# A macaron block on one core: the second FFN's down product partly by seven block products, and the gates' sigmoids moved to the reading back

## The chip, the cores and the metric

The kernel runs on one core of a Trainium2 chip. The core has a matrix engine (TensorE, PE in the profile, with its weight loads as PEld), VectorE (DVE), ScalarE (ACT), GpSimd (POOL) and SyncE (SP, which here only issues DMAs). Each engine works through its own list of instructions in order; semaphores between the lists make one wait for another. The metric is the time of one execution on the device in microseconds (us). Three runs of the kernel before gave 1213.32, 1214.26 and 1214.87 us; the median is 1214.26.

## The reference

One block for x of 512 tokens by 1024 channels, all in float32:

```python
x = x + 0.5 * swiglu(rmsnorm(x, norm_ffn1_g), ffn1_w_gu, ffn1_w_down)
x = x + hybrid_mixer(rmsnorm(x, norm_mix_g), w_in, conv_w, ...)
x = x + 0.5 * swiglu(rmsnorm(x, norm_ffn2_g), ffn2_w_gu, ffn2_w_down)
return rmsnorm(x, final_norm_g)

def swiglu(x, w_gu, w_down):
    g, u = jnp.split(x @ w_gu, 2, axis=-1)
    return (jax.nn.silu(g) * u) @ w_down        # 1024 -> 2 x 2816 -> 1024
```

The mixer projects x by w_in into the parts of a short convolution (cb, cc, cu), of a gated linear attention (q, k, v, a low-rank gate, r) and into two gates ga and gb. It ends with

```python
merged = jax.nn.sigmoid(ga) * y_conv + jax.nn.sigmoid(gb) * y_gla
return merged @ w_o
```

## The kernel before

**Precision.** Every float32 product is made of three products in the type fp32r: a value is split into a high part (a cast on ScalarE) and a low part (value minus high part, a subtraction on VectorE), and high·high, high·low and low·high are summed. So every tile of weights costs a cast (L292) and a subtraction (L293), 128x1024 each, before TensorE can use it, and activations are split in the same way.

**Weights.** The class `Weights` (L226) streams all weights in the order of two tables: PLAN lists units (blocks of a matrix, at most 128x1024 in one tile), STEPS says which unit is used when. A unit is loaded into a pool `f` of 10 buffers by a DMA on SP's queue (L266); it is cast and subtracted into the pools `wh` and `wl` (3 buffers each) two steps before its use. The last four units (TAIL) go into buffers of the pool `op` instead, which has 14.

**Sets.** A large product is done in sets: a 2x2 block product by seven block products instead of eight (a Strassen-Winograd form). Their names, in the order in which a set takes them, are m1, p2, q6, p5, q7, p4, p3; where sets follow one another, the next set's first products are put between the last ones of this set (`order`, L80). Each set's weights are four loaded units a11, a12, a21, a22 and a fifth buffer s3. Sums of them are made in place: s3 = a11 + a21 on VectorE (L279), and a21 += a22, a11 += a21, a12 += a11 by accumulating DMAs that GpSimd issues (L270), the first three steps ahead of m1, the others right behind the casts for m1 and p2. Set loads are issued six steps ahead. The activations' side (class `Operands`, L493) has seven operands of 128x1024: four of them sums made in place on VectorE (L512 to L519), each cast (L532) and subtracted (L533) into two `op` buffers. `Set.run` (L470) makes one product: 24 matmuls 128x256 (L484) into one of three banks. The products m1, q6, q7 and p4 accumulate in the same bank b, p2 in a, p5 and p3 in c; after m1, q6 and q7 ScalarE copies bank b out (L489).

**FFN2.** The up product is units of its own for the first pairs, then nine sets. After sets 0 to 7 TensorE transposes x back to tokens-by-channels (`natural`, L678). Then `last_down` (L686): for each of 22 k tiles (128 rows of the down matrix, one unit of 128x1024) 4 token blocks by 2 column halves by 3 products, 528 matmuls 128x512 in all (L699 to L701), which accumulate in 8 banks over all k. The hidden activations are split two k tiles at a time (`split_hid`, L644: cast L648, subtraction L649). The last four k tiles go block by block, with the residual, the final norm and the store after each (`part`, `store`).

**Mixer gates.** ga and gb are made by four sets among the twelve sets of w_in (MSETS, L122). When a quarter of one is done it is put together from banks and copies (`quarter`, L1139; for p4 straight from the bank), a sigmoid is taken on ScalarE (L1163; for p4 L1158), and it is stored to DRAM by a DMA that ScalarE issues (L1170). Later `gate` (L1210) reads it back by a DMA on SP's queue: ga for the eight outputs of w_out_conv (`for d in range(KD)`, L1230), gb for the two sets of w_out_gla. The attention's gate and the set of r need other functions on ScalarE (L908 to L929; Silu for r), and a change of function can need a load of a table (ACT_TABLE_LOAD).

A scheduler sets each engine's order from the program's order and estimated times, except in the last token blocks, where the order is written by hand (L756).

Of the kernel before, what the change touches and what calls it, by code (L numbers as in the profile page):

```python
# [15 lines left out]
P = 128  # L16
S = 512
# [45 lines left out]
def full(mat, kt):  # L63
    return [(mat, k, 1, (0,), 1024) for k in range(kt)]
# [58 lines left out]
         ("conv", 3), ("cb", 0), ("cb", 1), ("r", 0), ("r", 1)]  # L123


def ffn_plan(up, down, plain, slow):

    units(group(up, KD, (0, DFF, P, DFF + P), slow))
    for f in range(2, plain):
        units(single(up, KD, f * P))  # L130
        units(single(up, KD, DFF + f * P))
    sets(up, [(s * HW, DFF + s * HW) for s in range(plain // 2, KF // 2)])
    units(full(down, KF))
    ENDS.append(len(STEPS))


# [30 lines left out]
def block_kernel(ctx: ExitStack, tc: tile.TileContext, xT, vecs, gf, gup, wgl, wts, out):  # L167
# [371 lines left out]
    def run_sets(make, ahead=2, hooks={}):  # L539


        at = W.taken
        seq = []
        while STEPS[at + len(seq)][1] is not None:
# [12 lines left out]

    def ffn(up, down, norm, nxt, plain, at):
# [6 lines left out]

        o = mm_group(up, KD, (0, DFF, P, DFF + P), xh, xl, extra=finish, slow=nxt is not None)
        row = rows[0]
        xn = {}

        def normed(j, l):  # L570

            if (j, l) not in xn:
                t = slice(l * HW, (l + 1) * HW)
                v = tile_of("hid", [P, 1024]).rearrange("p (k t) -> p k t", t=HW)
# [10 lines left out]
        hid = []  # L585

        def plain_pair(f, g, u):
            if f % 2 == 0:
                hid.append(tile_of("hid", [P, 2, S]))
# [17 lines left out]
            plain_pair(f, g, u)  # L607

        def up_set(i):
            h = tile_of("hid", [P, 2, S])  # L610
            hid.append(h)

            def done(s, p):
                bank, v = s.bank, s.v
# [36 lines left out]

        us = full(down, KF)
        if nxt is None:
            return last_down(us, split_hid)
        o = [AUX(), AUX()] + [MM() for _ in range(KD - 2)]

        def mm(d, k, w, hl):
# [28 lines left out]
    def last_down(us, split_hid):  # L686
        X = XS[-1]
        gr = []
        for e in range(2):
            g = acc_row.tile([P, S], F32, tag=("acc", "row")[e], name=f"gr{e}")  # L690
# [5 lines left out]
        def mm(t, e, k, w, hl):  # L696
            wh, wl = (a[:, 512 * e : 512 * (e + 1)] for a in w)
            a, b = (v[:, k % 2, t * P : (t + 1) * P] for v in hl)
            nc.tensor.matmul(o[t][e], a, wh, start=k == 0, stop=False)  # L699
# [75 lines left out]
    def mixer(norm, nxt):  # L775
# [377 lines left out]
        def act_done(func, use):  # L1153

            def done(s, p):
                if p == "p4":
                    t = T()
                    nc.scalar.activation(t, s.bank["b"], func, scale=-1.0)  # L1158
                else:
                    t = quarter(s, p)  # L1160
                    if t is None:
                        return
                    nc.scalar.activation(t, t, func)  # L1163
                use(int(p in ("p4", "q7")), int(p in ("q7", "p3")), t)
            return done

        def gate_done(name, i):
            def use(a, l, t):
                d = 4 * i + 2 * a
                nc.scalar.dma_start(  # L1170
                    gates_d[name][d : d + 2, :, half(l)].rearrange("e p t -> p e t"), pair(t))
            return act_done(AF.Sigmoid, use)

        def r_done(i):
            def use(a, l, t):
# [34 lines left out]
        def gate(name, d, l=None, t=None):  # L1210

            t = T() if t is None else t
            if l is None:
                nc.sync.dma_start(t, gates_d[name][d])
            else:
                nc.sync.dma_start(pair(t), gates_d[name][d : d + 2, :, half(l)].rearrange(
                    "e p t -> p e t"))
            return t

        c_h, c_l = parts([Y[i][:, :, 2:] for i in range(4)])  # L1220
# [141 lines left out]
```

## Time and profile before

| | |
|---|---|
| time, median of three runs | 1214.26 us |
| span of the profiled execution | 1213.3 us |
| PE busy | 1198.3 us (99% of the span) |
| DVE busy | 788.4 us (65%) |
| ACT busy | 591.4 us (49%) |
| POOL busy | 94.9 us (8%) |
| DMA, read and written | 124.55 MB and 8.39 MB, 110 GB/s over the span |
| ScalarE's table loads | 1.28 us each |

The trace has the times of one execution; that span is 1213.3 us, and the median of the runs, which also takes in what lies around a span, is 1.0 us more. Matmuls overlap, so the duration of one (0.39 us for 128x512) is not what it costs; its cost is the distance from one start to the next. Instructions on DVE and ACT overlap by some 0.09 us in the same way.

### The profile page before, as it was taken

The page shows a single profiled execution, that of the slowest core. Times are in us where ns is not written, and L with a number is a line of the kernel's source. Part 1 is how long each engine was busy: PE and PEld are TensorE (multiplying, and loading weights), DVE is VectorE, ACT ScalarE, POOL GpSimd, SP SyncE. Part 2 cuts the span into 40 slices and gives each one's busy share as a digit, 9 for nine tenths or more (in the row PEclk, how much of TensorE's full clock was granted, in tenths as well). Part 3 has the DMA queues.
Part 4 walks back from the last instruction along what each step waited for, and adds up shares of the span by engine and source line. Part 5 has one row for each costly group of instructions (what it writes and reads, how often), then busy time and mean ns, then how long its engine had stood idle before and what let it go on. Part 6 is the DMA issues. An engine that isn't in the chain of part 4 may idle for free.

```text
span 1213.3 us, 19084 instructions
## 1 busy us (share of the span) xinstructions
PE 1198.3 (99%) x7882; PEld 1103.2 (91%) x7882; DVE 788.4 (65%) x944; ACT 591.4 (49%) x733; POOL 94.9 (8%) x131
## 2 busy tenths in 40 slices
PE   9999999999999999999999999999999999999997
PEld 7899999988888889998999998988889999998886
DVE  7976666732277765666778778676597656583325
ACT  6555455532154465857555463444356545562323
POOL 0011111000010000010101100200001111100000
PEclk9999999999999999998999999999999999999999
DMA  9477776521162326765777756751537777752201
GB/s 343 98 198 189 178 192 177 174 88 61 52 243 86 95 64 165 205 159 144 199 191 178 191 168 208 202 163 67 184 89 199 181 184 170 184 186 88 70 1 70
DMA packets 57767, 184.51 MB, mean 152 GB/s; under 512 B 6384, under 2 KB 12656, under 8 KB 57680
## 3 DMA queue, kind: packets, MB, share of 16 engines
q1 hardware_dynamic: 37936, 124.27, 29.0%
q0 software_dynamic: 15104, 54.53, 24.3%
q10 hardware_dynamic: 4640, 4.49, 1.1%
q8 instruction: 61, 1.00, 0.3%
q14 instruction: 26, 0.21, 0.1%
HBM read 124.55 MB, written 8.39 MB: 110 GB/s over the span
## 4 chain that ended last, share of the span: by engine, by line
PE 95%; DMA 2%; DVE 1%; ACT 1%; issue 1%; SPq 0%; POOL 0%; ACTq 0%; DVEq 0%; POOLq 0%
PE mm L484 50%; PE mm L344 7%; PE mm L322 6%; PE mm L320 6%; PE mm L321 6%; PE mm L701 2%; PE mm L699 2%; PE mm L700 2%; PE mm L362 1%; PE mm L363 1%; PE mm L361 1%; DMA f<-f 1%; PE aux L701 1%; PE aux L322 1%; PE aux L320 1%; PE aux L699 1%
## 5 line engine op out<-in xcount | busy, mean ns | idle before, releaser
L484 PE MATMUL mm<-op,wh 128*128 128x256 f32 x3584 | 652.1, 285 | 3.0 <-ACT tp L489 2.5
L292 ACT CAST wh<-f 128x1024 fp32r<-128x1024 f32 (+1 forms) x313 | 326.9, 1046 | 502.4 <-PE mm L484 218.8
L484 PEld LDWEIGHTS mm<-op,wh 128*128 128x128 f32 x3584 | 562.6, 193 | 4.3 <-ACT tp L489 2.7
L293 DVE TENSOR_TENSOR wl<-f,wh 128x1024 fp32r<-128x1024 f32 (+1 forms) x313 | 380.6, 1218 | 284.8 <-ACT wh L292 274.0
L484 PE MATMUL mm<-op,wl 128*128 128x256 f32 x1792 | 509.6, 285 | 2.6 <-DVE wl L293 2.5
L484 PEld LDWEIGHTS mm<-op,wl 128*128 128x128 f32 x1792 | 345.4, 193 | 3.0 <-DVE wl L293 3.0
L270 POOL DMA_DIRECT2D f<-f x96 | 82.9, 863 | 827.4 <-DVE wl L293 471.8
L320 PE MATMUL mm<-op,wh 128*128 128x512 f32 x324 | 126.5, 390 | 0.0
L322 PE MATMUL mm<-op,wl 128*128 128x512 f32 x324 | 126.3, 390 | 0.0
L321 PE MATMUL mm<-op,wh 128*128 128x512 f32 x324 | 126.1, 389 | 0.0
L322 PEld LDWEIGHTS mm<-op,wl 128*128 128x128 f32 x324 | 60.8, 188 | 12.7
L321 PEld LDWEIGHTS mm<-op,wh 128*128 128x128 f32 x324 | 60.9, 188 | 12.6
L320 PEld LDWEIGHTS mm<-op,wh 128*128 128x128 f32 x324 | 60.8, 188 | 12.4
L344 PE MATMUL mm<-op,wh 128*128 128x512 f32 x256 | 63.7, 391 | 0.6 <-DVE op L395 0.3
L344 PEld LDWEIGHTS mm<-op,wh 128*128 128x128 f32 x256 | 47.7, 188 | 11.4 <-ACT wh L292 0.9
L489 ACT COPY tp<-mm 128x512 f32<-128x512 f32 x96 | 55.6, 580 | 4.6 <-PE mm L484 4.6
L699 PE MATMUL mm<-wh,op 128*128 128x512 f32 x108 | 42.0, 389 | 0.0
L700 PE MATMUL mm<-wl,op 128*128 128x512 f32 x108 | 42.0, 389 | 0.0
L701 PE MATMUL mm<-wh,op 128*128 128x512 f32 x108 | 42.0, 389 | 0.0
L279 DVE TENSOR_TENSOR f<-f,f 128x1024 f32<-128x1024 f32 x32 | 39.2, 1224 | 0.8
L649 DVE TENSOR_TENSOR op<-hid,op 128x1024 fp32r<-128x1024 f32 x22 | 26.9, 1222 | 17.7 <-ACT op L648 17.7
L344 PE MATMUL mm<-op,wl 128*128 128x512 f32 x128 | 34.4, 390 | 0.0
(252 smaller groups left out, 1129.0 us busy)
## 6 DMA issues: line engine op xcount, KB each, us to landing
f<-wts SPq DMA_DIRECT2D x219, 512.0 KB, 4.1
f<-f POOLq DMA_DIRECT2D x96, 512.0 KB, 4.9
X<-xT SPq DMA_DIRECT2D x8, 256.0 KB, 6.1
xs<-X POOLq DMA_DIRECT2D x8, 256.0 KB, 5.6
ga<-tp ACTq DMA_DIRECT2D x8, 256.0 KB, 2.7
gb<-tp ACTq DMA_DIRECT2D x8, 256.0 KB, 4.0
g<-gb SPq DMA_DIRECT2D x8, 256.0 KB, 5.0
tp<-ga SPq DMA_DIRECT2D x8, 256.0 KB, 5.9
```

The costliest lines, as they stand in the source:

```text
L270: nc.gpsimd.dma_start(out_, a, accum_op=ALU.add)
L292: nc.scalar.copy(h[:, :w], raw[:, :w])
L293: nc.vector.tensor_tensor(out=l[:, :w], in0=raw[:, :w], in1=h[:, :w].bitcast(F32), op=ALU.subtract)
L320: nc.tensor.matmul(o, wh, ah, start=first, stop=False)
L321: nc.tensor.matmul(o, wh, al, start=False, stop=False)
L322: nc.tensor.matmul(o, wl, ah, start=False, stop=last)
L344: nc.tensor.matmul(o[c], w[:, s : s + P], a[k], start=k == 0 and j == 0, stop=k == kt - 1 and j == 2)
L484: nc.tensor.matmul(to, ww[:, s], aa[:, t], start=fresh and k == 0 and e == 0 and j == 0, stop=k == 3 and j == 2, skip_group_check=True)
L489: nc.scalar.copy(v, o)
L699: nc.tensor.matmul(o[t][e], a, wh, start=k == 0, stop=False)
L700: nc.tensor.matmul(o[t][e], a, wl, start=False, stop=False)
L701: nc.tensor.matmul(o[t][e], b, wh, start=False, stop=k == KF - 1)
```

## The change

Two things. First, k tiles 0 to 15 of FFN2's down product are done by two sets (`wide_sets`), each over 8 k tiles, both column halves and all 512 tokens. A block is 4 k tiles by 512 columns by 256 tokens; as it has twice the size of a block in the other sets, each of the seven products takes two units of weights and 24 matmuls 128x512, and accumulates in two banks of 128 tokens each. 2 x 7 x 24 = 336 matmuls stand where 16 x 24 = 384 stood. The set's results are halved and summed straight into x: ScalarE copies bank b out with a factor of 0.5 after m1, q6 and q7 (L756 of the new kernel), VectorE adds the second bank (L759, L764, L773) or adds to x itself (L769), and GpSimd adds the sum into x (L761, L766, L775). k tiles 16 to 21 stay as they were. The products here come in the order of SEQ, without another set's products between. The pool of hidden activations is divided otherwise: two buffers of 16 KB a partition for the wide sets, three of 4 KB.

Second, the gates ga and gb are stored without their sigmoid (for p4 a Copy with scale -1 remains), and `gate` takes it after the reading back, in place.

```diff
+WIDE = 2
+SEQ = ("m1", "p2", "q6", "p5", "q7", "p4", "p3")
+def wide_sets(mat):
+    for w in range(WIDE):
+        subs = []
+        for u in range(2):
+            subs.append(len(PLAN))
+            PLAN.extend((mat, 8 * w + 4 * j + 2 * u, 2, (512 * c,), 512)
+                        for c in range(2) for j in range(2))
+        for p in SEQ:
+            STEPS.extend((n, p) for n in subs)
...
-    units(full(down, KF))
+    if not slow:
+        wide_sets(down)
+    units(full(down, KF)[0 if slow else 8 * WIDE :])
...
+        def run_wide(w):
+            ops = Operands(lambda j, l: wides[w][:, 4 * j : 4 * j + 4, l * HW : (l + 1) * HW])
+            bank, v = {}, {}
+            for at, p in enumerate(SEQ):
+                for q in SEQ[at : at + 2]:
+                    ops.make(q)
...
+                o = bank[b]
+                bh, bl = ops.get(p)
+                for u in range(2):
+                    h, l = W.take()
+                    for i in range(2):
+                        k = 2 * u + i
+                        wh, wl = (a[:, i * 512 : (i + 1) * 512] for a in (h, l))
+                        for t in range(2):
...
+                for t in range(2):
+                    if p in ("m1", "q6", "q7"):
+                        v.setdefault(p, []).append(T())
+                        nc.scalar.activation(v[p][t], o[t], AF.Copy, scale=0.5)
+                    if p == "p2":
+                        y, x_ = v["m1"][t], block(0, 0)[:, t]
+                        nc.vector.scalar_tensor_tensor(out=y, in0=o[t], scalar=0.5, in1=y,
+                                                       op0=ALU.mult, op1=ALU.add)
+                        nc.gpsimd.tensor_tensor(out=x_, in0=x_, in1=grid(y), op=ALU.add)
...
+                    if p == "p4":
+                        x_ = block(1, 0)[:, t]
+                        nc.vector.scalar_tensor_tensor(out=x_, in0=grid(o[t]), scalar=-0.5, in1=x_,
+                                                       op0=ALU.mult, op1=ALU.add)
...
-        for k in range(KF - TAIL):
+        K0 = 8 * WIDE
+        for k in range(K0, KF - TAIL):
...
-                    nc.scalar.activation(t, s.bank["b"], func, scale=-1.0)
+                    nc.scalar.activation(t, s.bank["b"], func or AF.Copy, scale=-1.0)
...
-                    nc.scalar.activation(t, t, func)
+                    if func is not None:
+                        nc.scalar.activation(t, t, func)
...
-            return act_done(AF.Sigmoid, use)
+            return act_done(None, use)
...
+            nc.scalar.activation(t, t, AF.Sigmoid)
             return t
...
-    FFN = dict(f=10, hid=11, tp=9)
+    FFN = dict(f=10, hidw=2, hid=3, tp=9)
```

Lines move: in the weights' class L292 and L293 become L310 and L311 and the GpSimd DMA L270 becomes L288; the operands' L532 and L533 become L550 and L551; the copy L489 becomes L507; in the mixer L1163, L1158 and L1170 become L1256, L1250 and L1263, and the new sigmoid is L1311.

The lists of instructions change in three places that the prediction speaks of. The first is ScalarE in the mixer's sets, where the second ga set is made beside the attention's gate. Before, from the copy of a bank on (`wh` are casts of weights, `tp` quarters of a gate, `g` and `sm` the attention's gate, `mm` and `aux` banks):

```order
L489 COPY tp_5217<-mm_5187 128x512
L292 CAST wh_5219<-f_4602 128x1024
L1158 ACT_TABLE_LOAD
L1158 ACTIVATE tp_5247<-mm_4911 128x512
L292 CAST wh_5253<-f_4862 128x1024
L1170 DMA ga<-tp_5247 128x2x256
L292 CAST wh_5283<-f_4866 128x1024
L925 ACT_TABLE_LOAD
L925 ACTIVATE sm<-g_506_3628 128x8
L1163 ACT_TABLE_LOAD
L1163 ACTIVATE tp_5311<-tp_5311 128x512
L926 ACT_TABLE_LOAD
```

The same place after the change:

```order
L507 COPY tp_5204<-mm_5174 128x512
L310 CAST wh_5206<-f_4593 128x1024
L1017 ACT_TABLE_LOAD
L1017 ACTIVATE sm<-g_497_3623 128x8
L1018 ACTIVATE sm<-g_497_3623 128x8
L1019 ACTIVATE g_500_3626<-g_498_3624 128x512
L1250 ACTIVATE tp_5234<-mm_4900 128x512
L310 CAST wh_5240<-f_4851 128x1024
L1263 DMA ga<-tp_5234 128x2x256
L1020 ACTIVATE g_498_3624<-g_498_3624 128x512
L310 CAST wh_5270<-f_4855 128x1024
```

Three table loads of this stretch are gone, and the sigmoid of a ga quarter with them; one table load stands between the first two casts of weights still, and the attention's gate has moved forward.

The second place is ScalarE from the end of the last r set to the first outputs of w_out_conv. Before (L1202 casts the convolution's result, L532 the attention's):

```order
L489 COPY tp_7053<-mm_6870 128x512
L292 CAST wh_7059<-f_6610 128x1024
L1202 CAST op_7177<-y_3402 128x1024
L1163 ACTIVATE tp_7055<-tp_7055 128x512
L292 CAST wh_7099<-f_7091 128x1024
L1163 ACTIVATE tp_7088<-tp_7088 128x512
L292 CAST wh_7132<-f_7093 128x1024
L1158 ACTIVATE tp_7128<-mm_6870 128x512
```

After, the first gb gate's sigmoid comes ahead of the copy, and again some rows on, ahead of the weights of the fourth output (the second fence):

```order
L1311 ACT_TABLE_LOAD
L1311 ACTIVATE g_497_3623<-g_497_3623 128x512
L507 COPY tp_7036<-mm_6853 128x512
L310 CAST wh_7042<-f_6593 128x1024
L1295 CAST op_7160<-y_3397 128x1024
L1256 ACT_TABLE_LOAD
L1256 ACTIVATE tp_7038<-tp_7038 128x512
L1256 ACTIVATE tp_7071<-tp_7071 128x512
L310 CAST wh_7082<-f_7074 128x1024
```

The rows that follow four rows later, still on ScalarE (two sigmoids of ga after one of gb and one Silu of r):

```order
L1311 ACT_TABLE_LOAD
L1311 ACTIVATE g_499_3625<-g_499_3625 128x512
L1256 ACT_TABLE_LOAD
L1256 ACTIVATE tp_7144<-tp_7144 128x512
L1311 ACT_TABLE_LOAD
L1311 ACTIVATE tp_7173<-tp_7173 128x512
L1311 ACTIVATE tp_7220<-tp_7220 128x512
L310 CAST wh_7226<-f_7080 128x1024
```

Sigmoids that wait for a reading back, and the changes of table between them and the Silu of r, now stand ahead of casts of weights; before the change there was no table load here.

The third place is ScalarE in the first wide set, around the evacuation of q7 (`hidw` is the set's block of hidden activations; L550 casts its operands):

```order
L310 CAST wh1502_10961<-f1434_10558 128x1024
L550 CAST op1534_11151<-hidw1186_8664 128x1024
L310 CAST wh1506_10982<-f1426_10518 128x1024
L310 CAST wh1508_11000<-f1433_10556 128x1024
L550 CAST op1536_11156<-hidw1186_8664 128x1024
L756 ACTIVATE tp1510_11016<-mm1462_10796 128x512
L756 ACTIVATE tp1511_11020<-mm1463_10797 128x512
L310 CAST wh1514_11030<-f1424_10514 128x1024
```

VectorE at that place:

```order
L311 TENSOR_TENSOR wl1507_10983<-f1426_10518,wh1506_10982 128x1024
L532 SCALAR_TENSOR_TENSOR hidw1186_8664<-hidw1186_8664 128x4x256
L311 TENSOR_TENSOR wl1509_11001<-f1433_10556,wh1508_11000 128x1024
L537 SCALAR_TENSOR_TENSOR hidw1186_8664<-hidw1186_8664 128x4x256
L764 SCALAR_TENSOR_TENSOR tp1510_11016<-mm1488_10925,tp1510_11016 128x512
L764 SCALAR_TENSOR_TENSOR tp1511_11020<-mm1489_10926,tp1511_11020 128x512
L311 TENSOR_TENSOR wl1515_11031<-f1424_10514,wh1514_11030 128x1024
```

Before, this stretch held a cast and a subtraction of one unit for each k tile and a `split_hid` for every two. Now the two copies of bank b (mm1462 and mm1463) stand on ScalarE behind the cast of an operand (op1536), whose input the sum L532 on VectorE makes; TensorE's product p4 writes the same two banks.

More of the change, by code (lines that the diff above doesn't have):

```diff
@@ L543, in run_sets @@
         seq = []
-        while STEPS[at + len(seq)][1] is not None:
+        while STEPS[at + len(seq)][1] is not None and PLAN[STEPS[at + len(seq)][0]][4] == HW:
             seq.append(STEPS[at + len(seq)])
@@ L567, in ffn @@
         row = rows[0]
-        xn = {}
+        xn, xn_tile = {}, []
         def normed(j, l):
@@ L573, in normed @@
                 t = slice(l * HW, (l + 1) * HW)
-                v = tile_of("hid", [P, 1024]).rearrange("p (k t) -> p k t", t=HW)
+                if not xn:
+                    xn_tile.append(tile_of("hidw", [P, 4, 4, HW]))
+                v = xn_tile[0][:, len(xn)]
                 for i in range(4):
@@ L585, in ffn, with new_hid @@
         hid = []
+        wides = []
+        def new_hid():
+            i = len(hid)
+            if i < 4 * WIDE:
+                if i % 4 == 0:
+                    wides.append(tile_of("hidw", [P, 8, S]))
+                hid.append(wides[-1][:, 2 * (i % 4) : 2 * (i % 4) + 2])
+            else:
+                hid.append(tile_of("hid", [P, 2, S]))
+            return hid[-1]
         def plain_pair(f, g, u):
             if f % 2 == 0:
-                hid.append(tile_of("hid", [P, 2, S]))
+                new_hid()
             s, t = T(), T()
@@ L609, in up_set @@
         def up_set(i):
-            h = tile_of("hid", [P, 2, S])
-            hid.append(h)
+            h = new_hid()
             def done(s, p):
@@ L653, in ffn @@
         if nxt is None:
-            return last_down(us, split_hid)
+            return last_down(us, split_hid, wides)
         o = [AUX(), AUX()] + [MM() for _ in range(KD - 2)]
@@ L684, in natural, with last_down, block, grid @@
         nc.scalar.copy(X[:, i], o)
-    def last_down(us, split_hid):
+    def last_down(us, split_hid, wides):
         X = XS[-1]
+        def block(c, l):
+            return X[:, 4 * c : 4 * c + 4, l * HW : (l + 1) * HW].rearrange(
+                "p d (t i) -> p t d i", i=P)
+        def grid(t):
+            return t.rearrange("p (d i) -> p d i", i=P)
+        def run_wide(w):
[4 more added lines that the diff above has]
+                    ops.make(q)
+                b = {"m1": "b", "p2": "a", "q6": "b", "p5": "c", "q7": "b", "p4": "b",
+                     "p3": "c"}[p]
+                fresh = b not in bank
+                if fresh:
+                    bank[b] = [MM(), MM()]
+                o = bank[b]
[6 more added lines that the diff above has]
+                        for t in range(2):
+                            s = slice(k * HW + t * P, k * HW + (t + 1) * P)
+                            nc.tensor.matmul(o[t], bh[:, s], wh, start=fresh and k == 0,
+                                             stop=False, skip_group_check=True)
+                            nc.tensor.matmul(o[t], bh[:, s], wl, start=False, stop=False,
+                                             skip_group_check=True)
+                            nc.tensor.matmul(o[t], bl[:, s], wh, start=False, stop=k == 3,
+                                             skip_group_check=True)
+                for t in range(2):
[7 more added lines that the diff above has]
+                        nc.gpsimd.tensor_tensor(out=x_, in0=x_, in1=grid(y), op=ALU.add)
+                    if p == "q7":
+                        y, x_ = v["q7"][t], block(1, 1)[:, t]
+                        nc.vector.scalar_tensor_tensor(out=y, in0=bank["c"][t], scalar=0.5, in1=y,
+                                                       op0=ALU.mult, op1=ALU.add)
+                        nc.gpsimd.tensor_tensor(out=x_, in0=x_, in1=grid(y), op=ALU.subtract)
+                    if p == "p4":
+                        x_ = block(1, 0)[:, t]
+                        nc.vector.scalar_tensor_tensor(out=x_, in0=grid(o[t]), scalar=-0.5, in1=x_,
+                                                       op0=ALU.mult, op1=ALU.add)
+                    if p == "p3":
+                        y, x_ = v["q6"][t], block(0, 1)[:, t]
+                        nc.vector.scalar_tensor_tensor(out=y, in0=o[t], scalar=0.5, in1=y,
+                                                       op0=ALU.mult, op1=ALU.add)
+                        nc.gpsimd.tensor_tensor(out=x_, in0=x_, in1=grid(y), op=ALU.add)
+        for w in range(WIDE):
+            run_wide(w)
@@ L698, in mm @@
             a, b = (v[:, k % 2, t * P : (t + 1) * P] for v in hl)
-            nc.tensor.matmul(o[t][e], a, wh, start=k == 0, stop=False)
+            nc.tensor.matmul(o[t][e], a, wh, start=k == K0, stop=False)
             nc.tensor.matmul(o[t][e], a, wl, start=False, stop=False)
             nc.tensor.matmul(o[t][e], b, wh, start=False, stop=k == KF - 1)
-        for k in range(KF - TAIL):
+        K0 = 8 * WIDE
+        for k in range(K0, KF - TAIL):
             if k % 2 == 0:
```

## The prediction

> **What bounds the kernel now.** I read the page's busy times first, then its chain of work that ended last, then what TensorE waited for, then a table of windows for the two stages in which the wide sets will lie.
>
> ```profile
> PE 1198.3 (99%) x7882; PEld 1103.2 (91%) x7882; DVE 788.4 (65%) x944; ACT 591.4 (49%) x733; POOL 94.9 (8%) x131
> PE 95%; DMA 2%; DVE 1%; ACT 1%; issue 1%; SPq 0%; POOL 0%; ACTq 0%; DVEq 0%; POOLq 0%
> ```
>
> TensorE is busy 99% of the span, and the chain runs 95% through it. So a matmul that goes is worth its distance to the next one, and work on another engine costs only where TensorE comes to wait for it.
>
> ```profile
> PE mm L484 <- DVE wl L293: 2.5, 1, 2.5
> PE mm L484 <- ACT tp L489: 2.5, 1, 2.5
> PE aux L956 <- DVE qk L458: 0.7, 1, 0.7
> PE mm L484 <- ACT wh L292: 0.5, 1, 0.5
> ```
>
> These are TensorE's waits (total, times, longest, in us). There are two large ones, 2.5 us each, and both lie in the mixer: none is in FFN2. The stages of FFN2, in the windows' table (for each engine its busy time and count, then the granted clock, the DMAs' share and GB/s):
>
> ```profile
> core 0: us, PE busy (x) PEld busy (x) DVE busy (x) ACT busy (x) POOL busy (x), PEclk, DMA share, GB/s
> 901.00:1086.20 185.20, 185.20 (x1546) 185.12 (x1545) 127.18 (x128) 102.07 (x126) 21.34 (x25) 1.00 0.72 183
> 1086.20:1206.20 120.00, 120.00 (x531) 99.05 (x529) 46.17 (x65) 35.55 (x49) 0.00 (x0) 1.00 0.18 59
> ```
>
> The first window is the up sets, the second the down product. In the second TensorE is the only bound: VectorE works 46 of 120 us, GpSimd not at all.
>
> **The change part by part.**
>
> *Matmuls.* 120.00 us by 531 matmuls is 0.226 us for one 128x512. 336 stand where 384 stood, so 48 x 0.226 = **-10.9 us**. The stage of 16 k tiles goes from 384 x 0.226 = 86.8 to 75.9 us, 38.0 for each set. The shape of a matmul stays, and each works from the same kinds of tiles, so I leave its price.
>
> *VectorE in a wide set.* Durations overlap, so starts are what counts:
>
> ```profile
> 886.39 1.21 DVE L293 TENSOR_TENSOR wl<-f,wh 128x1024 fp32r<-128x1024 f32 x1
> 887.52 1.22 DVE L533 TENSOR_TENSOR op<-hid,op 128x1024 fp32r<-128x1024 f32 x1
> 888.65 0.68 DVE L458 TENSOR_TENSOR hid<-tp,tp 128x512 f32<-128x512 f32 x1
> 889.26 1.22 DVE L293 TENSOR_TENSOR wl<-f,wh 128x1024 fp32r<-128x1024 f32 x1
> ```
>
> A 128x1024 takes 1.13 us from start to start (887.52 to 888.65), a 128x512 0.61. A set has 14 low parts of weights, 2 sums s3, 7 low parts of operands and 4 operand sums, 27 x 1.13 = 30.5, and 8 evacuations, 8 x 0.61 = 4.9: 35.4 us, beside 38.0 of TensorE. VectorE goes from some 40% to 93% of the stage. That leaves 2.6 us in a set, so TensorE keeps its bound only just, and only if what it needs comes in the right order.
>
> *ScalarE in a wide set.* 14 casts of weights, 7 of operands, 6 copies:
>
> ```profile
> 553.82 1.05 ACT L292 CAST wh<-f 128x1024 fp32r<-128x1024 f32 x1
> 554.89 1.28 ACT L1158 ACT_TABLE_LOAD   x1
> 556.18 0.60 ACT L1158 ACTIVATE tp<-mm 128x512 f32<-128x512 f32 x1
> 556.67 1.04 ACT L292 CAST wh<-f 128x1024 fp32r<-128x1024 f32 x1
> 557.61 1.05 ACT L292 CAST wh<-f 128x1024 fp32r<-128x1024 f32 x1
> ```
>
> A cast takes 0.94 from start to start, a 128x512 0.49: 21 x 0.94 + 6 x 0.49 = 22.7 us. It is not the bound, but one place of its order is. Products q7 and p4 follow each other in the same two banks, so p4 waits for ScalarE's copies of q7. In the first set these stand behind the cast of an operand (op1536), which waits for the sum L532 on VectorE; in the up sets another set's product lies between. Following both lists with the times above, TensorE waits 1.2 us in the first set and 0.9 in the second, where another cast stands between the copies: 2.1 us. If the copies stood first it would be 0.25 each, 0.5 in all, since the second bank's copy (0.6 us) runs beside the first matmuls of the first bank. Elsewhere the lists leave low parts 0.5 to 2 us ahead of their use; at 93% some of these will fail, for which I add 1.0 us a set. **+4.1 us**, between 0.5 and what GpSimd may do to it.
>
> *GpSimd's adds.* 12 adds of 128x512, 6 a set, each in SBUF. No elementwise work of this kind is in the trace; the nearest rows are
>
> ```profile
> L817 POOL MEMSET sc<- 128x512 f32 x1 | 0.5, 546 | 0.0
> L316 POOL CAST ones_r<-ones 128x128 fp32r<-128x128 f32 x1 | 0.3, 289 | 0.0
> f<-f POOLq DMA_DIRECT2D x96, 512.0 KB, 4.9
> ```
>
> The memset gives 0.55 us for 128x512; the cast's 0.289, four times, gives 1.16; with two operands to read, twice that, 2.3. Nothing waits for the sums themselves until the last blocks. Behind them on GpSimd's queue stand the accumulating DMAs of the second set's weights (4.9 us to landing each, two in a row), which by the lists have about 4 us to spare, so adds up to 2.3 us cost nothing there. What is open is whether VectorE is slowed while GpSimd adds. In the trace no VectorE instruction stands beside such an add. Bounds: nothing, or VectorE held for the whole of each, 6 x 1.16 = 7.0 us a set, which makes it 42.4 against 38.0 and the wait 2 x 4.4 = 8.8. In the up sets VectorE's 1.13 us hold beside 25 GpSimd instructions, so I take the low end, no slowing.
>
> The Trainium skill speaks against that: its page "SBUF — State Buffer", section "Who interferes with whom", has the two engines share one port pair as an exclusive lock, which a VectorE instruction with two SBUF inputs takes against a GpSimd one that reads SBUF, and the second of them blocks. From "GPSIMD Engine Reference", section 3.1 (4497 ns for an add of 2048), my estimate of one add is 1.12 us, and the wait by it would be 2 x (35.4 + 6.7 - 38.0) = 8.2 us; no run here shows it.
>
> *Loads.* The wide units replace equal bytes on SP's queue; hidden tiles take the same space. Four casts of the last units move into this stage (their low parts, 4 x 1.13, fall in the second set, which is part of the 1.0 us). The end is left as it was.
>
> *The stall at 555.* Six table loads stood among ScalarE's casts.
>
> ```profile
> 554.92 0.51 PE L484 MATMUL mm<-op,wh 128*128 128x256 f32 x2 [0.48 <-ACT wh L292]
> 557.95 0.58 PE L484 MATMUL mm<-op,wl 128*128 128x256 f32 x1 [2.53 <-DVE wl L293]
> 558.00:560.00 2.00, 2.00 (x9) 2.00 (x10) 2.00 (x3) 1.97 (x3) 0.07 (x1) 0.50 0.28 90
> 560.00:562.00 2.00, 2.00 (x12) 2.00 (x11) 0.77 (x1) 1.47 (x2) 0.79 (x1) 0.50 0.34 66
> 562.00:564.00 2.00, 2.00 (x11) 2.00 (x11) 0.94 (x2) 0.22 (x1) 0.00 (x0) 0.50 1.14 156
> ```
>
> TensorE waited 0.48 + 2.53, then ran 6 us at a clock of 0.50. 32 matmuls are recorded there; at the up sets' 185.20 / 1546 = 0.120 us they take 3.8, so 2.2 went, or 3.0 by the clock; I take 2.7. In all 5.7 us. In the new order two of those table loads remain, and the casts of weights come some 3 us earlier, more than the 2.53. **-5.7 us**; if the stall stays, 0.
>
> *The stall at 808.* A copy stood behind a cast that waited for a DMA:
>
> ```profile
> 806.45 1.04 ACT L292 CAST wh<-f 128x1024 fp32r<-128x1024 f32 x1 [4.28 <-DMA f<-f]
> 807.41 0.58 ACT L489 COPY tp<-mm 128x512 f32<-128x512 f32 x1
> 808.04 0.50 PE L484 MATMUL mm<-op,wh 128*128 128x256 f32 x2 [2.49 <-ACT tp L489]
> 808.00:810.00 2.00, 1.96 (x16) 1.97 (x17) 2.00 (x4) 0.93 (x1) 0.00 (x0) 1.00 0.20 43
> ```
>
> After the change the copy stands ahead of that cast, but behind the sigmoid of a gb gate that was read back. That costs up to 0.5 us; most of 2.49 goes. The clock stayed at 1.00 here, so nothing more is in it. **-2.2 us.**
>
> *New waits on ScalarE, 715 to 760.* The sigmoids now wait for readings back, and casts of weights stand behind them.
>
> ```profile
> 715.47 0.38 SPq L1216 DMA_DIRECT2D g<-gb  x1
> 733.76 0.42 SPq L1216 DMA_DIRECT2D g<-gb  x1
> g<-gb SPq DMA_DIRECT2D x8, 256.0 KB, 5.0
> tp<-ga SPq DMA_DIRECT2D x8, 256.0 KB, 5.9
> 743.65 1.06 ACT L292 CAST wh<-f 128x1024 fp32r<-128x1024 f32 x1 [0.22 <-DMA g<-gb]
> ```
>
> First: issued at 715.47, landed by about 720, then table 1.28, sigmoid 0.63 and copy of q7 0.58 to 722.4. p4, which began at 721.7, loses 0.6. Second: Silu's table and two Silus stand ahead of the first output's weights; by the list the low part comes about 1.2 us late. Third: issued at 733.76, landed at 738.5, then sigmoid, table, Silu, table and two sigmoids, 0.63 x 4 + 1.28 x 2 = 5.1, to 743.6; the cast and low part of the fourth output are ready at 745.3, some 1.0 us after its low part is wanted. **+2.8 us**, from 0 (if the waits ahead move the need later) to 8 (if a reading back takes twice its 5 us).
>
> Elsewhere the gates' sigmoids lie beside full stretches of TensorE and cost nothing either way.
>
> *The sum.* -10.9 + 4.1 - 5.7 - 2.2 + 2.8 = -11.9 us. 1213.3 - 11.9 = 1201.4 us of span; the median lies 1.0 above the span, so **1202.4 us**.
>
> **The rivals.**
>
> *VectorE becomes the bound in the wide sets* through GpSimd, with an add of 1.16 us: 8.8 in place of 4.1 gives 1207.1. For it: 93% without any slowing. Against it: 1.13 us hold beside GpSimd's DMAs. The port rule above gives this result. Chance 0.18.
>
> *The gates' readings become the bound of the mixer*: one landing 5 us late, in front of casts of weights, gives 1207.4; a half clock behind it is in the price of the stall at 555 (2.7), not in this one. For it: six sigmoids in a row wait for DMAs. Against: the median 5.0 and 5.9. Chance 0.13.
>
> *Slower: GpSimd's adds at 2.3 us, with VectorE held for each.* The wait is 12 x 2.3 less the 2 x 2.6 that VectorE has to spare, 22.4 us, in place of 4.1: 1220.7. Without any wait the wide sets and gates give -16.0, so it needs 16.0 + 2.4 = 18.4 us of wait to be slower by 0.2%, which is an add of (18.4 + 5.2) / 12 = 2.0 us: between the row's 1.16 and its double. For it: two operands, and a four-dimensional view of x. Against: the memset's 0.55. Chance 0.08.
>
> *Better: the orders fit.* 0.5 in the wide sets, no new wait in the mixer, the 808 stall gone whole: -10.9 + 0.5 - 5.7 - 2.5 = -18.6, so 1195.7. Against it: ScalarE's order around q7. Chance 0.15.
>
> That the change doesn't do what it says can't be in the matmuls, whose number is counted.
>
> **How the numbers follow.** The forecast with its own range (1198.5 to 1206) has 0.46. The range from 1194.5 to 1212 takes in the better case and both dearer ones and leaves out the slower rival and the tails, about 0.17. A difference under 0.2% (2.4 us) can't be told from no change. Forecast, better case and the two middle rivals are faster by more, save for tails of 0.05 that end within: faster 0.87, same 0.06, slower 0.07.
>
> **What would show it.** In the new profile TensorE has no wait and no clock of 0.50 near 555; no 2.5 us wait near 808 at a copy; three short waits between 720 and 746 (for a copy, then twice for a low part). In the wide sets VectorE is busy over 90%, and TensorE waits once a set at p4 for L756. GpSimd's L761, L766 and L775 give the price of an add, and VectorE's 1.13 us beside them says whether it is held. Waits spread over many low parts in the wide sets, of 4 us or more a set, or adds of 2 us, would make the prediction wrong; so would half clock in the mixer after one of the new waits.

## The result, and the profile after

The changed kernel takes 1207.33 us (median of 4 runs, 1202.91 to 1208.01), the kernel before 1214.57 (4 runs): a ratio of 0.9936, with an interval of [0.9920, 0.9952], 7.2 us less. The forecast was 1202.4, 12 us less: the sign was right, the size 5 us too large. The profiled span is 1205.6 us.

The page's busy times and its chain of the new kernel:

```profile
PE 1187.8 (99%) x7834; PEld 1092.1 (91%) x7834; DVE 840.7 (70%) x990; ACT 612.1 (51%) x762; POOL 130.0 (11%) x155
PE 89%; DVE 4%; DMA 3%; issue 2%; ACT 1%; POOL 0%; SPq 0%; DVEq 0%; ACTq 0%; POOLq 0%
```

The chain now goes through VectorE for 4% of the span and through TensorE for 89% in place of 95%: there is a stage in which VectorE decides. TensorE's waits say where (total, times, longest):

```profile
PE mm L502 <- ACT tp L507: 3.3, 3, 1.8
PE mm L747 <- ACT wh L310: 2.4, 1, 2.4
PE mm L749 <- DVE wl L311: 2.0, 4, 0.9
PE mm L747 <- ACT tp L756: 1.7, 1, 1.7
```

L747 to L751 are the wide sets' matmuls. Before the change FFN2 had no wait; now it has six in the wide sets.

The starts of a few matmuls cut both traces into stages. In us, here and in the experiments below ("to conv" is from the span's start to the first matmul of w_out_conv, so it ends with the mixer's sets; "gla" from there to the first matmul of w_o; "up" from there to the last transpose after an up set; "step" from there to the first wide or down matmul; "down" from there to TensorE's end):

| | to conv | gla | up | step | down |
|---|---|---|---|---|---|
| before | 727.3 | 86.6 | 254.8 | 17.7 | 119.9 |
| after | 718.9 | 87.8 | 254.8 | 18.3 | 119.0 |

So the stages up to w_out_conv gave 8.4 us (0.8 of it before the first matmul of the mixer's sets, where nothing was changed, so the sets gave 7.6), gla took back 1.2, and the down product, which had lost 48 matmuls (10.9 us), gave 0.9, of which the step before it took back 0.6. Without waits the down stage would be 119.9 - 10.9 = 109.0 us.

**Where the 10.9 us went.** VectorE and GpSimd in the timeline of the new kernel (start, duration):

```profile
1091.83 1.28 DVE L759 SCALAR_TENSOR_TENSOR tp<-mm,tp 128x512 f32<-128x512 f32 x2
1093.02 1.95 DVE L311 TENSOR_TENSOR wl<-f,wh 128x1024 fp32r<-128x1024 f32 x1
1094.90 3.45 DVE L551 TENSOR_TENSOR op<-hidw,op 128x1024 fp32r<-128x1024 f32 x2
1098.27 1.21 DVE L311 TENSOR_TENSOR wl<-f,wh 128x1024 fp32r<-128x1024 f32 x1
1092.59 3.53 POOL L761 TENSOR_TENSOR X<-X,tp 128x512 f32<-128x512 f32 x2 [1.72 <-DVE tp L759]
```

Two adds on GpSimd lie from 1092.59 to 1096.12. The two subtractions that VectorE starts in that time and the one behind them take from 1093.02 to 1098.27, 5.25 us, where three took 3.4 in the up sets: 1.85 us more for one pair of adds. Over the six pairs of adds eleven subtractions are held so, and take together 10.0 us more than 1.22 us each, in a stage in which VectorE had, by the prediction's count, 2.6 us to spare in a set.

The largest of the waits comes at the end of the second set, on ScalarE and TensorE:

```profile
1139.01 1.04 ACT L310 CAST wh<-f 128x1024 fp32r<-128x1024 f32 x1
1147.28 1.04 ACT L310 CAST op<-f 128x1024 fp32r<-128x1024 f32 x1 [7.23 <-DMA f<-wts]
1148.23 1.04 ACT L310 CAST wh<-f 128x1024 fp32r<-128x1024 f32 x1
1149.33 0.50 PE L747 MATMUL mm<-wh,op 128*128 128x512 f32 x1 [2.35 <-ACT wh L310]
1150.77 0.50 PE L749 MATMUL mm<-wl,op 128*128 128x512 f32 x1 [0.95 <-DVE wl L311]
1152.00:1154.00 2.00, 2.00 (x6) 1.52 (x6) 2.00 (x2) 1.06 (x2) 0.00 (x0) 0.50 0.14 55
```

A cast into an `op` buffer, of one of the last four units, stands ahead of the cast (1148.23) that TensorE wants. It waits 7.23 us for its load, which was issued only about 1141, when VectorE had freed a buffer of pool f, late. TensorE waits 2.35 and 0.95 us, and then runs at a clock of 0.50 (the last row is a window of 2 us). The six waits make 6.1 of the 10.0 us between 119.0 and 109.0, the slow clock some 1.7 (0.57 over the 4 us from 1151); the rest stands in no wait of the list.

### The profile page after: what moved, and what is told of

Same layout as the page of the kernel before. It is cut to its first block, busy times and chain, and to the rows that moved or that the text cites. A ratio compares the mean times of both kernels' runs of the same rounds, so it can differ in the third digit from the quotient of the medians.

```text
span 1205.6 us, 19145 instructions
## 1 busy us (share of the span) xinstructions
PE 1187.8 (99%) x7834; PEld 1092.1 (91%) x7834; DVE 840.7 (70%) x990; ACT 612.1 (51%) x762; POOL 130.0 (11%) x155
## 4 chain that ended last, share of the span: by engine, by line
PE 89%; DVE 4%; DMA 3%; issue 2%; ACT 1%; POOL 0%; SPq 0%; DVEq 0%; ACTq 0%; POOLq 0%
PE mm L502 50%; PE mm L362 7%; PE mm L340 6%; PE mm L338 6%; PE mm L339 6%; DVE wl L311 2%; DMA f<-f 1%; PE mm L380 1%; PE mm L381 1%; PE mm L379 1%; DMA g<-gb 1%; DMA f<-wts 1%; PE aux L340 1%; PE aux L338 1%; PE aux L339 1%
## 5 line engine op out<-in xcount | busy, mean ns | idle before, releaser
L310 ACT CAST wh<-f 128x1024 fp32r<-128x1024 f32 (+1 forms) x325 | 339.6, 1046 | 483.6 <-PE mm L502 225.2
L311 DVE TENSOR_TENSOR wl<-f,wh 128x1024 fp32r<-128x1024 f32 (+1 forms) x325 | 400.4, 1235 | 242.0 <-ACT wh L310 230.2
L288 POOL DMA_DIRECT2D f<-f x108 | 93.3, 869 | 847.0 <-DVE wl L311 470.1
L340 PE MATMUL mm<-op,wl 128*128 128x512 f32 x324 | 126.4, 390 | 0.1
L507 ACT COPY tp<-mm 128x512 f32<-128x512 f32 x96 | 55.8, 581 | 1.2 <-DVE tp L1238 1.0
L747 PE MATMUL mm<-wh,op 128*128 128x512 f32 x112 | 44.4, 398 | 4.1 <-ACT wh L310 2.4
L749 PE MATMUL mm<-wl,op 128*128 128x512 f32 x112 | 45.0, 401 | 2.1 <-DVE wl L311 2.0
L297 DVE TENSOR_TENSOR f<-f,f 128x1024 f32<-128x1024 f32 x36 | 44.0, 1221 | 1.8 <-DMA f<-f 1.0
L751 PE MATMUL mm<-wh,op 128*128 128x512 f32 x112 | 44.2, 395 | 0.0
L551 DVE TENSOR_TENSOR op<-hidw,op 128x1024 fp32r<-128x1024 f32 x28 | 36.0, 1297 | 1.3 <-ACT op L550 1.3
L550 ACT CAST op<-hidw 128x1024 fp32r<-128x1024 f32 x28 | 29.1, 1047 | 11.0 <-DVE hidw L597 4.0
```

Source lines behind the costliest of these rows:

```text
L288: nc.gpsimd.dma_start(out_, a, accum_op=ALU.add)
L310: nc.scalar.copy(h[:, :w], raw[:, :w])
L311: nc.vector.tensor_tensor(out=l[:, :w], in0=raw[:, :w], in1=h[:, :w].bitcast(F32), op=ALU.subtract)
L340: nc.tensor.matmul(o, wl, ah, start=False, stop=last)
L507: nc.scalar.copy(v, o)
L747: nc.tensor.matmul(o[t], bh[:, s], wh, start=fresh and k == 0, stop=False, skip_group_check=True)
```

## The experiments

Each comparison was made against runs of the kernel before on the same chip (medians 1213.7 to 1214.2). Line numbers of a variant may differ by a few from the new kernel's. The time is the median of the runs; the stages are those of the one execution that was profiled:

| | time, us | ratio to before | to conv | gla | down |
|---|---|---|---|---|---|
| wide sets alone | 1212.30 | 0.9985 [0.9975, 0.9995] | 723.7 | 88.2 | 117.8 |
| gates alone | 1209.72 | 0.9969 [0.9958, 0.9980] | 719.1 | 89.2 | 119.9 |
| no adds | 1202.45 | 0.9906 [0.9889, 0.9923] | 719.0 | 92.2 | 111.0 |
| adds by DMA | 1209.99 | 0.9967 [0.9955, 0.9979] | 718.5 | 88.0 | 118.3 |
| adds on VectorE | 1202.49 | 0.9908 [0.9893, 0.9922] | 719.0 | 90.8 | 110.5 |
| ScalarE in program order | 1212.00 | 0.9973 [0.9956, 0.9990] | 719.7 | 92.2 | 118.4 |
| adds by DMA, ScalarE in program order | 1207.16 | 0.9948 [0.9927, 0.9969] | 719.4 | 91.0 | 115.5 |
| ga only on reading back | 1211.36 | 0.9974 [0.9960, 0.9988] | 723.9 | 85.7 | 119.1 |
| QS for E | 1203.13 | 0.9908 [0.9891, 0.9925] | 718.8 | 84.5 | 118.0 |
| QS for E, adds on VectorE | 1195.66 | 0.9846 [0.9832, 0.9861] | 718.0 | 84.2 | 110.1 |
| wide sets alone, adds on VectorE | 1206.17 | 0.9937 [0.9922, 0.9952] | 725.2 | 88.6 | 110.1 |
| gates alone, QS for E | 1204.56 | 0.9919 [0.9900, 0.9939] | 718.5 | 85.4 | 119.9 |

**The two parts apart.** The wide sets with the gates as they were:

```diff
-            return act_done(None, use)
+            return act_done(AF.Sigmoid, use)
...
-            nc.scalar.activation(t, t, AF.Sigmoid)
             return t
```

> The wide sets alone, the gates as before. In the traces of before and after the last landmark ahead of the wide sets (the transposes after the up sets) lies 7.2 us earlier after the change, and the end 7.5 us earlier. Theory 1, the parts add up and the wide sets earn only those 0.3 us: 1213.5 to 1215 us. Rival, the wide sets earn their 10.9 us less some 4 us of waits whenever the mixer is as before: 1206 to 1209 us.

And the gates' part put into the kernel before, which keeps `full(down, KF)`:

> The gates' part alone, the down product as before. Theory 1: all but 0.3 us of the gain comes from the mixer: 1207 to 1208.5 us, no wait and no half clock near 555, one wait of about 1 us near 713 and one of about 2 us near 782. Rival, forecast's size: 5.1 us, 1209.5 us; rival, gates no gain of their own: 1214.5 us.

The wide sets earn 1.4 us by the medians (1212.30 beside 1213.69); the rival that they earn some 7 in a mixer as before falls, and theory 1's 1213.5 to 1215 is missed by 1.2 on the other side. The gates earn 4.0, less than the 7 of theory 1 and near the rival of the forecast's size, 5.1: the wait near 782 was 3.2 us in this trace and 1.8 in the changed kernel's. The down stage shows the wide sets' 2.1 us and the gates' none.

The wide sets alone reach w_out_conv at 723.7 us, 3.6 earlier than the kernel before, though their gates are the same. TensorE's waits there are the same too (0.77, 0.49 and 2.53 us, where before had 0.75, 0.48 and 2.53), but no half clock follows them. The last of these waits, and a window behind it:

```profile
556.99 0.38 PE L502 MATMUL mm<-op,wl 128*128 128x256 f32 x1 [2.53 <-DVE wl L311]
558.00:560.00 2.00, 2.00 (x19) 2.00 (x18) 1.88 (x3) 1.97 (x3) 0.86 (x1) 1.00 0.04 8
```

From the first matmul of the mixer's sets to that of w_out_conv it is 275.7 us in the trace of before, 271.6 in this one and 268.1 in the changed kernel's. So of the 7.6 us that the sets gave between the two profiled executions, 4.1 hang on the half clock of the execution before, which another one with the same waits did not have; 3.5 are left for the waits themselves.

**Are GpSimd's adds the cause?** One kernel leaves them out:

```diff
-                        nc.gpsimd.tensor_tensor(out=x_, in0=x_, in1=grid(y), op=ALU.add)
```

(and the one with subtract in the same way).

> The twelve GpSimd adds into x are left out, so part of the residual sum is missing. Theory 2, GpSimd's adds hold VectorE (two of its instructions beside each pair of adds take 1.95 to 2.3 us in place of 1.22, about 1.9 us a pair, 11 us in all), and the waits for low parts, the late last load and the half clock after it follow from that: all VectorE instructions of 128x1024 in the wide sets take 1.22 us, the waits for low parts and the wait of 2.35 us near 1149 are gone, 1.2 to 2 us of waits for the copies of q7 stay, 1199.5 to 1202 us. Rival, the order of ScalarE's list makes these waits (a cast of a tail unit ahead of a wide unit's, the copies of q7 behind an operand's cast): VectorE gets faster but the time stays at 1205.5 to 1207.5 us.

The down stage falls from 119.0 to 111.0 us, 2.0 above the 109.0 that the matmuls need. The groups of VectorE's subtractions in the wide sets, of the changed kernel and then of this one (busy, mean ns):

```profile
L311 DVE TENSOR_TENSOR wl<-f,wh 128x1024 fp32r<-128x1024 f32 x27 | 38.4, 1435 | 0.0
L551 DVE TENSOR_TENSOR op<-hidw,op 128x1024 fp32r<-128x1024 f32 x11 | 15.4, 1414 | 0.0
```

```profile
L311 DVE TENSOR_TENSOR wl<-f,wh 128x1024 fp32r<-128x1024 f32 x28 | 34.1, 1224 | 3.9 <-ACT wh L310 3.6
L551 DVE TENSOR_TENSOR op<-hidw,op 128x1024 fp32r<-128x1024 f32 x11 | 13.3, 1224 | 0.0
```

1435 and 1414 ns become 1224, and VectorE now has idle time before the first group. The waits for low parts and that of 2.35 us are gone; only those for the copies of q7 stay (1.4 us in two). ScalarE and VectorE have the same lists in this stage as in the changed kernel, in the same order. So it is the adds and not the order, and the late load was their consequence. The whole time fell only by 5 us, to just above the range expected, since the wait near 782 was 5.0 us in this trace (below).

That could still be the adds as such and not where they run. So they were made on VectorE itself, with nothing left out:

```diff
-                        nc.gpsimd.tensor_tensor(out=x_, in0=x_, in1=grid(y), op=ALU.add)
+                        nc.vector.tensor_tensor(out=x_, in0=x_, in1=grid(y), op=ALU.add)
```

> The twelve adds on VectorE in place of GpSimd; nothing is left out. VectorE gets 6 x 0.61 = 3.7 us more in each set, 39.1 beside 38.0 of TensorE, but no hold of some 5.6 us a set. Theory 2: the stage from the first wide matmul to TensorE's end (119.0 us after the change, 111.0 without the adds) takes 113 to 116 us; 1202 to 1205 us. Rival, the order of the lists makes the waits: 118 to 119.5 us, 1206.5 to 1208 us.

The down stage is 110.5 us, less even than expected, and 1202.49 us in all. VectorE does more work and TensorE waits less: 0.7 us in the wide sets. The adds cost VectorE 12 x 0.6 = 7.3 us when it makes them, and 10.0 when GpSimd does. The scheduler has ordered both lists anew here, though (the copies of q7 stand ahead of the operand's cast), so the run doesn't part the adds' place from the new order; the runs without adds and, below, with adds by DMA keep the order.

**Is it the order of ScalarE's list?** The rival, with the list in the wide sets as the program has it:

```diff
-        for w in range(WIDE):
-            run_wide(w)
+        with tc.manual_schedule(engines={ENG.Activation}):
+            for w in range(WIDE):
+                run_wide(w)
```

> The change with ScalarE's list in the wide sets in the order of the program: the copies of q7 stand behind no operand's cast that waits, and the tail units' casts behind all wide units' casts. Nothing is left out. Rival of theory 2, the order of the lists makes the waits: the wait of 1.7 us for the copies and those of 2.4 and 0.95 us near 1150 with the half clock go, 113 to 115 us for the stage and 1202 to 1204 us. Theory 2: VectorE is the bound, held by the adds; the waits come back as waits for low parts, 117 to 119.5 us, 1205.5 to 1208 us.

The down stage keeps 118.4 us; the waits for q7's copies and for the tail's cast go, and others come: 2.5 us for an operand's low part, 1.5 for low parts of weights, 1.5 for casts. The stage is in theory 2's range, but this run alone does not decide. Four of the new waits, two of 0.73 us for casts and two of 0.77 for low parts of weights, stand with the same lengths at the same places in the last kernel of the next part, which has this order and no adds on GpSimd: they come from the order of the program itself. The rival falls by the kernel without adds. The time is worse than either expected, 1212.0, with runs from 1205.4 to 1215.0: the wait near 782 was 5.1 us in this trace.

**Adds by DMA.** GpSimd issues accumulating DMAs in place of its adds (for q7 the sign is put into the scale):

```diff
-                        nc.gpsimd.tensor_tensor(out=x_, in0=x_, in1=grid(y), op=ALU.add)
+                        nc.gpsimd.dma_start(x_, grid(y), accum_op=ALU.add)
```

> The twelve adds into x are made by accumulating DMAs that GpSimd issues, instead of by GpSimd itself; nothing is left out. Theory 2: as without adds, 1199.5 to 1203 us, as the DMAs take no time of VectorE. Rival, the order of the lists makes the waits: 1205.5 to 1207.5 us. A third way: the extra transfers, 12 of 256 KB, delay the accumulating DMAs of the weights on the same queue by more than the 4 us that they have to spare: over 1208 us, with waits for f in the second set.

VectorE's subtractions take 1221 ns with its list as in the changed kernel, so the hold is gone here too, but the down stage is 118.3 us: TensorE waits 4.2 us for a cast. That is the place of the tail unit's load again, late this time without a hold of VectorE. Theory 2's time fails; 1209.99 is the time of the third way, but that the adds' transfers delay the weights' accumulating DMAs is not shown. With ScalarE's list in program order as well:

> The adds as accumulating DMAs, and ScalarE's list in the order of the program. With the adds as DMAs the largest wait was 4.2 us for a cast that stood behind a tail unit's cast, whose load landed late. If that order is what the DMAs' version lost by: 111.5 to 114 us for the stage and 1201 to 1204 us. If the late loads themselves hold TensorE: 116 to 119 us, 1206 to 1210 us.

115.5 us for the stage, between the two ranges: the order explains 2.8 of the 9.3 us lost there, and 6.5 remain. 3.0 of them are the four waits of program order named above, 1.4 a wait for an operand's low part; the rest was not taken further.

**The mixer's new wait.** In the changed kernel, ScalarE, SP's queue and TensorE near 780:

```profile
772.00 0.38 SPq L1309 DMA_DIRECT2D g<-gb  x1
779.96 0.63 ACT L1311 ACTIVATE g<-g 128x512 f32<-128x512 f32 x1 [4.53 <-DMA g<-gb]
780.50 1.03 ACT L310 CAST wh<-f 128x1024 fp32r<-128x1024 f32 x1
781.43 0.58 ACT L507 COPY tp<-mm 128x512 f32<-128x512 f32 x1
782.06 0.50 PE L502 MATMUL mm<-op,wh 128*128 128x256 f32 x2 [1.84 <-ACT tp L507]
784.00:786.00 2.00, 2.00 (x11) 2.00 (x11) 1.93 (x3) 0.19 (x1) 0.00 (x0) 0.50 0.63 235
```

A reading of gb is issued at 772.00, when the tile E that it goes into is free, and lands 7.9 us later. Its sigmoid waits for it on ScalarE, and behind that stand the cast and the copy which TensorE wants. In the kernel before, the same reading took 10.0 us to land, and TensorE did not wait. Here it waits 1.84 us and runs at half clock behind it. First all of gb's sigmoids were put back to the storing:

```diff
-            return act_done(None, use)
+            return act_done(AF.Sigmoid if name == "gb" else None, use)
```

(and after the reading back a sigmoid only for ga).

> The change with gb's sigmoids taken before the storing, as before the change; only ga's are taken on reading back. Theory 3: the waits near 713 (1.1 us) and near 782 (1.8 to 5.0 us, with half clock behind it) come from gb's sigmoids, which wait on ScalarE for a reading back ahead of casts of weights and copies; so both are gone, and the stretch from the first w_out_conv to w_o takes under 86 us (87.8 after the change, 86.6 before). 1202.5 to 1205 us. Rival: gb's sigmoids bring their table loads back into the sets, and the stall near 555 or the one near 508 with them: 1206 to 1210 us.

Both halves happen. The gla stage falls to 85.7 us, under the 86 expected, and no wait is near 713 or 782 (one of 1.6 us for a copy is back near 804, the place of the stall at 808); but w_out_conv begins at 723.9 in place of 718.9, with a wait of 1.8 us near 505, for a cast, and half clock behind it. So the rival has the sum: 1211.36. Then the one tile was exchanged:

```diff
-                    sg[0, 0] = gate("gb", 4 * i, 0, E)
+                    sg[0, 0] = gate("gb", 4 * i, 0, QS if i else E)
```

> The change, but the second gla set's first gb gate is read into the tile QS in place of E, so that its reading back need not wait for the first set's last use of E; nothing is left out. Theory 3 (that reading, issued at 772 and landed near 780, holds ScalarE ahead of a cast and a copy, 1.8 to 5 us of TensorE and a half clock after it): the wait near 782 is gone, the stretch from the first w_out_conv to w_o takes 83.5 to 85 us (87.8 after the change), 1202.5 to 1205 us. Rival: the copy waits for something else behind it (the cast of a sum that GpSimd's DMA makes, as at 808 before the change): a wait of 2 us stays, 1206 to 1208 us.

The wait is gone, the gla stage takes 84.5 us and the whole 1203.13: 4 us for one tile. The reading's issue and its sigmoid (the second of the two in the row) now stand far ahead:

```profile
730.12 0.37 SPq L1309 DMA_DIRECT2D g<-gb  x1
734.87 1.14 ACT L1311 ACTIVATE g<-g 128x512 f32<-128x512 f32 x2
```

So the cause is shown: the reading back waited for E. How long TensorE then waited hung on the landing alone: in the seven traces with E the reading is issued between 771.8 and 772.8 and lands 7.9 to 11.1 us later, and TensorE's wait (1.8 to 5.1) is each time 6.0 us less than that. The median of the changed kernel's readings of gb is 3.8 us; why this one takes two to three times as long is open.

**Both mends, and each part with its mend.**

> Both: the twelve adds on VectorE, and QS in place of E. Theories 2 and 3 add up: 110 to 112 us for the wide stage to TensorE's end, 83.5 to 85 us from w_out_conv to w_o: 1196 to 1199 us. Rival: one gain hides the other's (a wait moves to the next place): 1200.5 to 1203 us, as with the adds alone.

> The wide sets alone with their adds on VectorE, the gates as before the change. If the wide sets are worth their matmuls once GpSimd does not hold VectorE, the stage takes 110 to 111.5 us in place of 119.9: 1213.9 less 9, 1204 to 1206 us. Rival: with the gates as before the stage comes with weights less far ahead, and waits return: over 1207 us.

> The gates' part alone with QS in place of E, the down product as before. Wide sets alone with adds on VectorE gave 8.0 us, both together 18.5. If the parts add up, the gates with QS alone are worth 10.5 us: 1203 to 1205 us, with no wait over 0.5 us from 500 to 815. Rival, they do not add up (the wide sets' gain needs the mixer's or the reverse): over 1206.5 us.

With both, 1195.66 us, 18.5 less than before and just under the range expected. TensorE's waits in that trace, all but the one at the program's start:

```profile
PE mm L502 <- ACT tp L507: 0.7, 2, 0.4
PE mm L747 <- ACT tp L756: 0.4, 1, 0.4
```

The wide sets alone with their adds on VectorE give 8.0 us (0.2 short of the range expected; the stage is 110.1), the gates alone with QS 9.2. That is 17.2 together, not quite the 18.5 of both, and the gates' value was expected 1.3 us higher. In gates alone with QS TensorE waited 0.7 us for an operand (L344) and 0.5 for a low part, where the combined kernel did not wait; the rest is within what the medians of before move by (1213.7 to 1214.2).

## Why the prediction was right and where not, point by point

*Matmuls, -10.9:* right. With the adds on VectorE or left out, the down stage is 110.1 to 111.0 us where it was 119.9, and TensorE's remaining waits there are 0.4 to 1.4 us.

*VectorE and ScalarE in a wide set, +4.1:* this step failed. The prediction counted 93% of the stage for VectorE and then, for the question "whether VectorE is slowed while GpSimd adds", took "the low end, no slowing". It took it from rows in which VectorE lay beside GpSimd's issues of DMAs: they could say nothing of an add. Measured, the wait and what follows it are 119.0 - 109.0 = 10.0 us in the down stage, near the first rival's 8.8 ("VectorE becomes the bound"). That rival had an add at 1.16 us and VectorE held for each, 2.3 a pair; the trace has 1.85 us held a pair, and adds of 1.3 us at least, 1.8 to 2.5 in the groups' means. The mechanism was the rival's, but the nearness of the sums is in part luck: up to the last wide matmul VectorE was held 9.2 us, which in the rival's own sum gives 2 x 35.4 + 9.2 - 2 x 38.0 = 4.0 us of wait. The rest of the 10.0 is not in that sum: 1.7 for the copies of q7, the late load, the slow clock behind it. The Trainium skill's lock rule on the page "SBUF — State Buffer", section "Who interferes with whom", agrees with what the trace shows for the subtractions, which have two SBUF inputs (1.22 us, up to 2.3 beside adds); the estimate of 8.2 us that the prediction made by it is near the 10.0 by the same luck. The estimate of one add from the Trainium skill's page "GPSIMD Engine Reference", section 3.1, 1.12 us, is below the 1.3 that the shortest one takes here.

*The copies of q7:* the mechanism was right, 1.72 us in the first set where 1.2 was worked out. In the second set this wait did not show. With the adds left out and the same order 1.1 us of it stayed, and 0.3 in the second set.

*The last units' casts:* they were counted as VectorE's time only. That a cast on ScalarE would wait for its load, ahead of a wide unit's cast, was not seen; with VectorE late it cost 3.3 us and a half clock.

*The stall at 555, -5.7:* it went, as forecast. But 2.7 of the 5.7 were the half clock of one execution; the wide sets alone have the same two waits at a full clock, so the 3.0 us of the waits are what both executions would save. The window of the new kernel has no wait and a full clock:

```profile
540.00:570.00 30.00, 30.00 (x252) 29.96 (x251) 26.58 (x37) 19.69 (x27) 3.99 (x5) 1.00 0.75 187
```

*A stall that the prediction listed and did not price.* It said that elsewhere the gates' sigmoids "cost nothing either way". The 0.7 us for qk in its first view of the waits lies at 506.90. In the kernel before, ScalarE there:

```profile
499.51 1.28 ACT L1163 ACT_TABLE_LOAD   x1
500.81 0.64 ACT L1163 ACTIVATE tp<-tp 128x512 f32<-128x512 f32 x1
501.46 1.28 ACT L927 ACT_TABLE_LOAD   x1
...
505.06 1.28 ACT L1158 ACT_TABLE_LOAD   x1
506.90 0.49 PE L956 MATMUL aux<-qk 128*128 128x128 f32 x2 [0.75 <-DVE qk L458]
508.00:512.00 4.00, 4.00 (x22) 3.54 (x22) 3.45 (x5) 2.78 (x4) 0.00 (x0) 0.69 0.55 147
```

They are gb's sigmoids and functions of the attention's gate, with a table load at each change; a clock of 0.69 followed from 508 to 512 (the last row). With the gates' sigmoids gone there, wait and slow clock are gone too; 0.75 us of wait and at least 1.2 of slow clock, most of what the sets gave beyond the forecast (7.6 in place of 5.7 less 0.6 for the first new wait, 5.1). The slow clock is again that of one execution: the wide sets alone have the wait, 0.77 us, and a clock of 1.00 from 508 to 512.

*The stall at 808, -2.2, and the new waits, +2.8:* the first went, as forecast. Of the three new waits the first came (1.10 us, at 713, where 0.6 was worked out; 0.3 or none in the other traces), the second was 0.3 in place of 1.2, the third did not come. But a fourth was missed: the prediction followed the sigmoids up to 760 and not those of the gla sets. It cost 1.84 us and a half clock in this trace, 1.9 to 5.1 us in others, and took back what 808 gave. It is what the second rival said in general (a landing some 5 us late in front of casts of weights), at a place where the prediction had not looked.

So the first rival in FFN2 and a better mixer than forecast gave the sum, 1207.3, within the range but not by the terms of the forecast. That it lies 0.2 us from this rival's 1207.1 is luck: FFN2 lost more than the rival said, and the mixer, in part by the clock of the execution profiled before, gave more.

## What to carry to other kernels

Before work is moved to an idle engine, ask what the busy engine pays for it: here GpSimd's adds took more of VectorE's time (10.0 us) than the adds themselves do there (7.3), so an engine that is at 8% busy was not free. A function that is moved behind a DMA makes everything behind it in its engine's list wait for that landing; look for what the DMA itself waits for, since a free tile in place of a used one was worth 4.2 us here, beside the 8.0 of the wide sets with their adds on VectorE. Where no row of the trace shows an effect, its price is open, not zero. And a half clock seen in one execution is no sure saving: look whether the next one with the same waits has it.

## What the runs showed of the hardware

Twelve adds of 128x512 on GpSimd took 1.3 to 4.0 us each, with group means of 1.8 to 2.5, and VectorE's two-input subtractions beside them went from 1.22 to as much as 2.3 us. The evacuations that read PSUM and one SBUF tile kept their 0.68 us: four lie for 0.45 us or more beside an add, and one (at 1157.14) wholly within the recorded time of one. Waits of TensorE were followed by half clock in some places (1.84 us at 782, 2.35 at 1149) and not in others (1.72 us at 1110, 2.49 at 808 in the kernel before), and a wait of 2.53 us near 557 was in one execution (before) and was not in another (the wide sets alone). The wait near 782 varied with the landing of one DMA between 1.8 and 5.1 us; the runs of the changed kernel spread over 5.1 us and those with both mends over 2.4.
